# FFN way down in halves of 256 columns, block by block, with h at another address, and a new order of the last normalisation

## Chip, core and metric

One Trainium2 core runs the whole kernel. The metric is the device time of one execution in microseconds; the kernel before takes 991.96 us, the median of 3 runs (991.29 to 992.9).

## The reference, cut to what matters

One block of a model: a half-weighted FFN, a mixer, a second half-weighted FFN and a final RMS norm, all in float32, with 512 tokens, D = 1024 and D_FF = 2816.

```python
def swiglu(h, w_gate, w_up, w_down):
    return (jax.nn.silu(h @ w_gate) * (h @ w_up)) @ w_down

x = x + 0.5 * swiglu(rmsnorm(x, norm_ffn1[l]), w_ffn1_gate[l], w_ffn1_up[l], w_ffn1_down[l])
x = x + hybrid_mixer(rmsnorm(x, norm_mix[l]), ...)          # two kinds of attention, not touched here
x = x + 0.5 * swiglu(rmsnorm(x, norm_ffn2[l]), w_ffn2_gate[l], w_ffn2_up[l], w_ffn2_down[l])
return rmsnorm(x, norm_final)
```

## The kernel before, in words

Every float32 product is made of three matmuls (`mm3`, lines 100 to 103): each operand is split into a high part and the rest, and high times high, high times rest and rest times high are summed in PSUM. ScalarE makes the high part (`halves` line 92, `halves_of_x` line 236), VectorE the rest (lines 96 and 237). Such a group of three is called a triple here. Each matmul has its own weight load.

An FFN has 22 blocks of 128 hidden features. The first four (`plain`) go through 24 matmuls of 512 columns for the gate and 24 for the up product. The other 18 go in nine pairs (`pair`), by a Winograd-like scheme on halves: 14 steps per pair, each of 12 matmuls of 256 columns into half of a PSUM bank (names pu, pv, pw), with additions of weights by VectorE in between. A hidden block is kept as h, high and rest, in 16 buffers of 128x512 (`kept`, lines 265 to 270).

The way down (`down`, line 392) multiplies four kept blocks by the down weights, for each of the 8 output blocks d: four triples of 512 columns into one bank pd, and then `half_added` (line 531) by VectorE into x. The first way down comes in two groups of four output blocks; the last one of the first FFN (two hidden blocks) in groups of 4, 2 and 2. The four ways down between are made while pairs run: `mixed` (line 442) lays one block d after every four or so pair steps, 28 steps to 8 blocks (14 to 8 for the last). There `run(d)` issues nothing itself: it puts its triples on the list `waiting`, and `between` (line 437) takes them off one by one, after each pair step and, when more than four wait, in the middle of one too (lines 340 and 341). `held` keeps the first five steps free of them. `issue_after(self.in_pair.ins)` (line 419) holds a triple behind the pair's matmuls on TensorE.

`go` (line 465) walks the steps: loads run 12 steps ahead, sums 6, halves 4. All weights are fetched by SyncE's queue. The order of instructions on each engine is planned ahead by the framework with a simulated timeline (line 1234), within data dependences and the `issue_after` edges; on the chip each engine keeps that order.

Addresses: tiles of a pool lie one behind the other, pools too. Nearly all have a multiple of 256 bytes per partition; a `gap` tile of 64 bytes (line 218) stands between th3/tl3 and the other tiles of `sp`. So the pairs' weights (sph, spl) lie 64 bytes higher modulo 256 than their moving operands (th3, tl3, xo), and the way down's weights (whi, wlo) and its moving h are equal modulo 256.

The end (lines 1112 to 1159): x is turned by TensorE to token-major z, four row tiles i in two halves of 512 columns. For each i and half there are two triples of the last two hidden blocks (h is the stationary operand here), then `residual`: VectorE adds into z, ScalarE squares it with a running sum into ss. GpSimd makes the mean's first half and multiplies z by the gain in the first half. `norm(i)` follows at once: Sqrt by ScalarE, reciprocal by VectorE, one half scaled by ScalarE, the other by VectorE, and two DMAs out on SyncE's queue.

Of the kernel before, what the change touches and what calls it, by code (L numbers as in the profile page):

```python
# [9 lines left out]
F32 = mybir.dt.float32  # L10
# [5 lines left out]
S = 512  # L16
# [5 lines left out]
FP = 4  # L22
# [7 lines left out]
def block_kernel(ctx: ExitStack, tc: tile.TileContext, A: dict, out: bass.AP):  # L30
# [69 lines left out]
    def mm3(p, w, v, first, last, again=False):  # L100
        nc.tensor.matmul(p, w[0], v[0], start=first, stop=False, skip_group_check=again)  # L101
        nc.tensor.matmul(p, w[0], v[1], start=False, stop=False, skip_group_check=again)  # L102
        return nc.tensor.matmul(p, w[1], v[0], start=False, stop=last, skip_group_check=again)  # L103

    def mm2(p, w, v, first, last):

# [21 lines left out]

    gates = cp.tile([128, NT, 24], F32, name="gates")
    pos = cp.tile([128, 2, 32], F32, name="pos")  # L130
    ss = cp.tile([128, 2, NT], F32, name="ss")
# [3 lines left out]
    cp.tile([128, 48], F32, name="rest")  # L135
# [56 lines left out]
    class Ffn:  # L192
# [26 lines left out]

# [87 lines left out]
        def pair(self, f):  # L307
# [36 lines left out]
            def copied(m, to, name):  # L344
                part[m, name] = self.sp.tile([128, HT], F32, name="wc", tag="wc", bufs=4)
# [43 lines left out]
                                  lambda m=m, then=then: then(m)])  # L389
            return steps  # L390

        def down(self, w, fs, then, tags=("mm",), groups=(1,) * NK, kept_back=True, left=None):


            n = len(fs)
            raw, got, bank = {}, {}, {}

            def loads(d):
                if d % (8 // n) == 0:
                    raw[d * n // 8] = chunk((8, 128))  # L400
                    fetch(raw[d * n // 8], w[d * n // 8])

            def halves_of(d):
                if d % (4 // n) == 0:
                    i = d * n % 8
                    with self.behind_lo() if kept_back else nullcontext():
                        parts = halves(raw[d * n // 8][:, i:i + 4])
                    for k, v in enumerate(parts):
                        got[d + k // n, k % n] = v

            def run(d):
                ds = {sum(groups[:g]): range(sum(groups[:g]), sum(groups[:g + 1])) for g in range(len(groups))}.get(d)
                if ds is None:
                    return

                def triple(i, k):
                    if k == 0:
                        bank[i] = pt(tags[i % len(tags)], "pd")
                    with tc.issue_after(self.in_pair.ins) if left != 0 and self.in_pair else nullcontext():
                        mm3(bank[i], got[i, k], self.hs[fs[k]], k == 0, k == n - 1)  # L420
                    if k == n - 1:
                        then(i, bank[i])
# [4 lines left out]
                at = 0 if left is None else len(todo) - (left if ds[-1] == NK - 1 else 0)  # L427
                if at:
                    self.between(len(self.waiting))
                for one in todo[:at]:  # L430
                    one()
# [5 lines left out]
        def between(self, n):  # L437

            for _ in range(min(n, len(self.waiting))):
                self.waiting.pop(0)()  # L440

        def mixed(self, steps, fills, tail=1):

# [8 lines left out]
        def lay(self, wd):  # L452

            for f in range(FP):
                self.steps += self.plain(f)
            self.steps += self.down(wd[0], range(FP), half_added, ("s", "t", "o", "mm"), (4, 4), False, 1)
            fills = []
            for f in range(FP, NF, FP):
                fs = range(f, min(f + FP, NF))
                pairs = [step for i in fs[::2] for step in self.pair(i)]  # L460
                self.steps += self.mixed(pairs, fills) if fills else pairs
                if len(fs) == FP:
                    fills = self.down(wd[f // FP], fs, half_added)

        def go(self, after):
            steps, at = self.steps, [0, 0, 0]
            late, count = None, 0
            for i, s in enumerate(steps):
# [20 lines left out]
            self.between(len(self.waiting))  # L489


    scr_t = dp.tile([16, 128, RVW], F32, name="scr_t")
# [40 lines left out]
    with ExitStack() as ph:  # L533
# [55 lines left out]
            squares(tmp, d, "tmp", 5)  # L589

        ffn.lay(A["wd1a"])
        ffn.steps += ffn.down(A["wd1b"], range(NF - NF % FP, NF), then, (None,), (4, 2, 2), left=0)
        ffn.go(after)


# [495 lines left out]
    with ExitStack() as ph:  # L1091
# [41 lines left out]
        def norm(i):  # L1133
            r = ss[:, 1, i:i + 1]
            nc.scalar.activation(r, r, AF.Sqrt, bias=mean[:, i:i + 1], scale=1.0 / D)
            nc.vector.reciprocal(r, r)
            y = [xp.tile([128, S], F32, name="xo", tag="xo", bufs=16) for _ in range(2)]
            nc.scalar.activation(y[0], z[i, 0], AF.Copy, scale=r)
            nc.vector.scalar_tensor_tensor(y[1], z[i, 1], r, gf[1], ALU.mult, ALU.mult)
            for half in range(2):  # L1140
                nc.sync.dma_start(out[i * 128:(i + 1) * 128, half * S:(half + 1) * S], y[half])

        last = range(NF - NF % FP, NF)
        w = [load(A["wd2b"][half]) for half in range(2)]
# [2 lines left out]
                z[i, half] = turn_x(i, half)  # L1147
        for i in range(NT):
            b = slice(i * 128, (i + 1) * 128)
            for half in range(2):  # L1150
                p = pt(None, "pd")
                for k, f in enumerate(last):
                    mm3(p, (hs[f][0][:, b], hs[f][1][:, b]), w[half][k], f == last[0], f == last[-1])
                residual(i, half, p)
                if half == 0:
                    nc.gpsimd.tensor_scalar(mean[:, i:i + 1], ss[:, 0, i:i + 1], 1.0 / D, 1e-6, ALU.mult, ALU.add)
                    nc.gpsimd.tensor_tensor(z[i, 0], z[i, 0], gf[0], ALU.mult)
                else:
                    norm(i)


def _buckets(dist):
# [84 lines left out]
```

## Time and profile before

| | us |
|---|---|
| median of 3 runs | 991.96 |
| the profiled execution | 990.21 |
| its span, first to last instruction | 988.4 |
| mean granted TensorE clock | 0.997 of full speed |
| HBM read and written | 97.98 MB and 5.30 MB |
| the way down between pairs, stage by stage | about 124 to 331 and 750 to 960 |

All rows come from one profiled execution. Times in them are microseconds from the first instruction. TensorE's matmuls are pipelined: the duration in a row includes the drain, so the cost of one in a stream is the distance of its start to the next start. "PE" is the matmul, "PEld" the weight load that runs beside it, "DVE" VectorE, "ACT" ScalarE, "POOL" GpSimd, "SPq" the queue of SyncE. The name pd<-h,whi reads: written pd, read h and whi.

### The profile page before, as it was taken

To read this page: it belongs to the slowest core of one execution; us is meant where nothing else is said; L and a number is where in the kernel's file an instruction comes from. 1 tells how busy PE (TensorE), PEld (TensorE's weight loads), DVE (VectorE), ACT (ScalarE), POOL (GpSimd) and SP (SyncE) were. 2 spreads that over 40 slices of the span, in tenths; PEclk is the share of its full clock that TensorE was granted. 3 is DMA by queue.
4 is the path that set the end of the run, shared out by engine and by line. 5 is a ranking of instruction groups with operands and counts; after the bars stand their busy time and mean duration, and the time that the engine had idled before them with its cause. 6 is when DMAs were issued, how large, how long until landed. Compare 5 with 4: busy or idle time off the path is not lost.

```text
span 988.4 us, 16902 instructions
## 1 busy us (share of the span) xinstructions
PE 970.5 (98%) x6084; PEld 859.0 (87%) x6084; DVE 778.5 (79%) x1579; ACT 561.9 (57%) x1165; POOL 132.5 (13%) x176
## 2 busy tenths in 40 slices
PE   9999999999999999999999999999999999999996
PEld 7789999999999898787878888888999999999985
DVE  6996997688776587768788978789898788777744
ACT  6464655445544366567677886655475445454435
POOL 0000000000000000035666676100000000000002
PEclk9999999999999999999999999999999999999998
DMA  7255534332321125531121232226254322341102
GB/s 257 97 185 173 196 129 133 110 102 91 97 68 43 58 88 190 181 113 33 53 72 43 87 85 80 71 86 213 67 166 153 119 73 95 101 128 44 54 11 86
DMA packets 50056, 104.52 MB, mean 106 GB/s; under 512 B 10129, under 2 KB 14690, under 8 KB 49972
## 3 DMA queue, kind: packets, MB, share of 16 engines
q1 hardware_dynamic: 49684, 102.91, 32.4%
q8 instruction: 48, 0.79, 0.3%
q10 hardware_dynamic: 288, 0.52, 0.1%
q14 instruction: 36, 0.29, 0.1%
HBM read 97.98 MB, written 5.30 MB: 104 GB/s over the span
## 4 chain that ended last, share of the span: by engine, by line
PE 91%; DVE 4%; issue 1%; ACT 1%; DMA 1%; POOL 0%; SPq 0%; POOLq 0%; ACTq 0%; DVEq 0%
PE pd L102 8%; PE pd L103 8%; PE pd L101 8%; PE pu L101 6%; PE pu L103 6%; PE pu L102 6%; PE pw L101 4%; PE pw L103 4%; PE pw L102 4%; PE pp L103 3%; PE pp L101 3%; PE pp L102 3%; PE pgu L102 3%; PE pgu L101 3%; PE pgu L103 3%; PE ps_t L940 3%
## 5 line engine op out<-in xcount | busy, mean ns | idle before, releaser
L236 ACT ACTIVATE sph<-aw 128x512 fp32r<-128x512 f32 x252 | 157.3, 630 | 197.4 <-PE pu L102 71.1
L237 DVE TENSOR_TENSOR spl<-aw,sph 128x512 fp32r<-128x512 f32 x252 | 172.3, 690 | 59.7 <-ACT sph L236 57.2
L92 ACT ACTIVATE whi<-raw 128x512 fp32r<-128x512 f32 (+1 forms) x200 | 121.5, 619 | 126.4 <-PE pd L102 44.2
L102 PE MATMUL pd<-h,whi 128*128 128x512 f32 x336 | 132.7, 395 | 0.0
L103 PE MATMUL pd<-h,wlo 128*128 128x512 f32 x336 | 131.1, 393 | 0.0
L96 DVE TENSOR_TENSOR wlo<-raw,whi 128x512 fp32r<-128x512 f32 (+1 forms) x168 | 111.7, 676 | 24.1 <-ACT whi L92 20.6
L101 PE MATMUL pd<-h,whi 128*128 128x512 f32 x336 | 130.4, 394 | 0.0
L101 PE MATMUL pu<-th,sph 128*128 128x256 f32 x432 | 119.4, 276 | 0.3 <-ACT wc L346 0.3
L103 PE MATMUL pu<-th,spl 128*128 128x256 f32 x432 | 119.4, 276 | 0.0
L102 PE MATMUL pu<-tl,sph 128*128 128x256 f32 x432 | 119.2, 276 | 0.0
L322 DVE TENSOR_TENSOR aw<-aw 128x512 f32<-128x512 f32 x144 | 99.0, 689 | 0.0
L531 DVE SCALAR_TENSOR_TENSOR x<-pd,x 128x512 f32<-128x512 f32 x88 | 60.1, 689 | 33.3 <-PE pd L103 33.3
L101 PEld LDWEIGHTS pu<-th,sph 128*128 128x128 f32 x432 | 81.1, 188 | 4.6 <-ACT wc L346 0.5
L102 PEld LDWEIGHTS pu<-tl,sph 128*128 128x128 f32 x432 | 81.1, 188 | 4.0
L103 PEld LDWEIGHTS pu<-th,spl 128*128 128x128 f32 x432 | 81.1, 188 | 0.1
L101 PE MATMUL pw<-xo,sph 128*128 128x256 f32 x288 | 79.7, 277 | 0.2 <-ACT sph L236 0.2
L102 PE MATMUL pw<-xo,sph 128*128 128x256 f32 x288 | 79.5, 276 | 0.0
L103 PE MATMUL pw<-xo,spl 128*128 128x256 f32 x288 | 79.4, 277 | 0.0
L103 PEld LDWEIGHTS pd<-h,wlo 128*128 128x128 f32 x336 | 63.1, 188 | 13.8
L102 PEld LDWEIGHTS pd<-h,whi 128*128 128x128 f32 x336 | 63.1, 188 | 4.0
L101 PEld LDWEIGHTS pd<-h,whi 128*128 128x128 f32 x336 | 63.1, 188 | 3.7
L101 PEld LDWEIGHTS pw<-xo,sph 128*128 128x128 f32 x288 | 54.1, 188 | 3.9 <-ACT sph L236 0.6
(246 smaller groups left out, 2443.1 us busy)
## 6 DMA issues: line engine op xcount, KB each, us to landing
aw<-in_wg SPq DMA_DIRECT2D x72, 256.0 KB, 2.8
aw<-in_wu SPq DMA_DIRECT2D x72, 256.0 KB, 4.5
raw<-in_wd1a SPq DMA_DIRECT2D x20, 512.0 KB, 3.9
raw<-in_wd2a SPq DMA_DIRECT2D x20, 512.0 KB, 4.8
raw<-in_w_a SPq DMA_DIRECT2D x16, 512.0 KB, 4.8
raw<-in_w SPq DMA_DIRECT2D x8, 512.0 KB, 4.0
raw<-in_w_o SPq DMA_DIRECT2D x8, 512.0 KB, 3.6
raw<-in_wg SPq DMA_DIRECT2D x7, 512.0 KB, 3.6
```

The costliest lines, as they stand in the source:

```text
L92: last_hi[0] = nc.scalar.activation(hi, v, AF.Copy)
L96: nc.vector.tensor_tensor(lo, v, f32(hi), ALU.subtract)
L101: nc.tensor.matmul(p, w[0], v[0], start=first, stop=False, skip_group_check=again)
L102: nc.tensor.matmul(p, w[0], v[1], start=False, stop=False, skip_group_check=again)
L103: return nc.tensor.matmul(p, w[1], v[0], start=False, stop=last, skip_group_check=again)
L236: nc.scalar.activation(hi, v, AF.Copy)
L237: self.last_lo = nc.vector.tensor_tensor(lo, v, f32(hi), ALU.subtract)
L322: nc.vector.tensor_tensor(to, x, y, op)
L531: nc.vector.scalar_tensor_tensor(xs[d], p, 0.5, xs[d], ALU.mult, ALU.add)
L940: nc.tensor.transpose(p[:, wide:wide + 128], lps[qi][:, j * 128:(j + 1) * 128], ident)
```

## The change

In `down`, a block of its own (the four ways down between the pairs) is now made at once, in two halves of 256 columns: for each half the four triples of that half, 24 matmuls where there were 12. `waiting`, `between`, `held` and `in_pair` are gone, so no triple stands inside or between pair steps other than in whole blocks. In `go` nothing is left over at the end. The first way down and the last one keep 512 columns and their groups; their banks are now taken from all four tags in turn.

A tile of 192 bytes (`gap_h`) ahead of h and one of 64 bytes (`gap_t`) ahead of th3/tl3 move h by 192 bytes modulo 256 and leave all else where it was modulo 256; `ss` grows and `rest` shrinks by as much. The way down's weights thereby lie 64 bytes higher modulo 256 than h, as the pairs' do.

At the end the second half of the last row tile is split in two parts of 256 columns, each with its own bank, residual and square; their sums meet in a small VectorE operation. `norm(i - 1)` is issued after the matmuls of tile i. Two edges hold a norm's reciprocal behind the newest residual, and its VectorE scaling behind that small sum. The very last first-half output goes out on ScalarE's queue.

```diff
@@ class Ffn, __init__
-            self.waiting = []
-            self.in_pair = None
-            self.held = 5
+            hp.tile([128, 48], F32, name="gap_h", tag="gap_h", bufs=1)
+            sp.tile([128, 16], F32, name="gap_t", tag="gap_t", bufs=1)
@@ pair, run
-                    self.in_pair = mm3(bank[m, to], (hi[:, k], lo[:, k]), x, first and k == 0, k == 3, not first)
-                    if k == 1:
-                        self.between(self.held == 0 and len(self.waiting) > 4)
-                self.between(self.held == 0)
-                self.held = max(self.held - 1, 0)
+                    mm3(bank[m, to], (hi[:, k], lo[:, k]), x, first and k == 0, k == 3, not first)
@@ down, run
-                todo = []
-                for ks in ([range(n)] if len(ds) == 1 else [range(n - 1), range(n - 1, n)]):
-                    todo += [lambda i=i, k=k: triple(i, k) for i in ds for k in ks]
...
-                self.waiting += todo[at:]
+                for i in ds:
+                    bank[i] = pt(tag, "pd")
+                if len(ds) == 1:
+                    for cols in (slice(0, HT), slice(HT, S)):
+                        for k in range(n):
+                            mm3(bank[d][:, cols], got[d, k], [v[:, cols] for v in self.hs[fs[k]]], k == 0, k == n - 1)
+                else:
+                    for ks in (range(n - 1), range(n - 1, n)):
+                        for i in ds:
+                            for k in ks:
+                                mm3(bank[i], got[i, k], self.hs[fs[k]], k == 0, k == n - 1)
+                for i in ds:
+                    then(i, bank[i])
@@ the end
-        def residual(i, half, p):
-            nc.vector.scalar_tensor_tensor(z[i, half], p, 0.5, z[i, half], ALU.mult, ALU.add)
-            nc.scalar.activation(sq, z[i, half], AF.Square, accum_out=ss[:, half, i:i + 1])
+        def residual(i, part, p, cols):
+            v = z[i, min(part, 1)][:, cols]
+            added[0] = nc.vector.scalar_tensor_tensor(v, p, 0.5, v, ALU.mult, ALU.add)
+            nc.scalar.activation(sq[:, cols], v, AF.Square, accum_out=ss[:, part, i:i + 1])
...
+            with tc.issue_after(added[0].ins):
+                nc.vector.reciprocal(r, r)
...
+            with tc.issue_after(summed_up[0].ins) if summed_up[0] else nullcontext():
+                nc.vector.scalar_tensor_tensor(y[1], z[i, 1], r, gf[1], ALU.mult, ALU.mult)
             for half in range(2):
-                nc.sync.dma_start(out[i * 128:(i + 1) * 128, half * S:(half + 1) * S], y[half])
+                queue = nc.scalar if i == NT - 1 and half == 0 else nc.sync
+                queue.dma_start(out[i * 128:(i + 1) * 128, half * S:(half + 1) * S], y[half])
...
+            parts = [slice(0, S), slice(0, S)] if i < NT - 1 else [slice(0, S), slice(0, S // 2), slice(S // 2, S)]
+            for part, cols in enumerate(parts):
+                p = pt(None, "pd")[:, cols]
...
+                residual(i, part, p, cols)
...
+                elif part < len(parts) - 1:
+                    summed_up[0] = nc.vector.scalar_tensor_tensor(
+                        mean[:, i:i + 1], ss[:, 1, i:i + 1], 1.0 / D, mean[:, i:i + 1], ALU.mult, ALU.add)
+            if i:
+                norm(i - 1, 1)
+        norm(NT - 1, 2)
```

## Rows read from the trace of the kernel before

**Rows 1.** The page, busy time of each engine over the span.
```profile
PE 970.5 (98%) x6084; PEld 859.0 (87%) x6084; DVE 778.5 (79%) x1579; ACT 561.9 (57%) x1165; POOL 132.5 (13%) x176
```
**Rows 2.** Busy time by stage: length, PE, PEld, DVE, ACT, POOL (count), clock, DMA share, GB/s.
```profile
124.00:331.00 207.00, 207.00 (x1461) 191.41 (x1460) 158.55 (x277) 100.63 (x194) 0.00 (x0) 1.00 0.30 94
712.00:750.00 38.00, 37.78 (x328) 37.45 (x327) 33.85 (x62) 25.69 (x52) 0.00 (x0) 1.00 0.45 149
750.00:960.00 210.00, 210.00 (x1475) 193.87 (x1474) 159.83 (x279) 100.03 (x194) 0.00 (x0) 1.00 0.27 89
```
**Rows 3.** Groups by line, TensorE, 124 to 331: shapes xcount | busy, mean ns | idle.
```profile
L102 PE MATMUL pd<-h,whi 128*128 128x512 f32 x116 | 46.1, 397 | 0.0
```
**Rows 4.** The same group from 750 to 960.
```profile
L102 PE MATMUL pd<-h,whi 128*128 128x512 f32 x120 | 47.7, 397 | 0.0
```
**Rows 5.** TensorE in order of time (start, duration), triples between steps of 256 columns.
```profile
302.80 0.40 PE L101 MATMUL pd<-h,whi 128*128 128x512 f32 x1
...
303.50 0.28 PE L101 MATMUL pv<-xo,sph 128*128 128x256 f32 x1
...
304.18 0.40 PE L101 MATMUL pd<-h,whi 128*128 128x512 f32 x1
```
**Rows 6.** TensorE in order of time, inside a long run of 512 columns.
```profile
690.74 0.39 PE L101 MATMUL pd<-h,whi 128*128 128x512 f32 x1
...
692.10 1.07 PE L101 MATMUL pd<-h,whi 128*128 128x512 f32 x4
```
**Rows 7.** TensorE in order of time, pairs alone, second FFN, and their first triple.
```profile
709.97 0.28 PE L103 MATMUL pw<-xo,spl 128*128 128x256 f32 x1
...
711.97 0.40 PE L101 MATMUL pd<-h,whi 128*128 128x512 f32 x1
...
713.46 0.28 PE L103 MATMUL pu<-th,spl 128*128 128x256 f32 x1
```
**Rows 8.** TensorE in order of time, a wait in the second FFN's pairs.
```profile
743.88 0.39 PE L101 MATMUL pu<-xo,sph 128*128 128x256 f32 x1 [0.22 <-ACT t L368]
744.10 0.28 PE L102 MATMUL pu<-xo,sph 128*128 128x256 f32 x1
...
745.28 0.28 PE L103 MATMUL pu<-xo,spl 128*128 128x256 f32 x1
```
**Rows 9.** TensorE in order of time, behind two waits in the first FFN's pairs.
```profile
109.70 0.28 PE L102 MATMUL pu<-tl,sph 128*128 128x256 f32 x1
...
110.84 0.28 PE L103 MATMUL pu<-th,spl 128*128 128x256 f32 x1
```
**Rows 10.** The end in order of time: TensorE's last matmul.
```profile
979.84 0.39 PE L103 MATMUL pd<-whi,h 128*128 128x512 f32 x1
```
**Rows 11.** The end in order of time: VectorE.
```profile
981.18 0.16 DVE L1136 RECIPROCAL ss<-ss 128x1 f32<-128x1 f32 x1 [0.64 <-ACT ss L1135]
981.26 0.67 DVE L1130 SCALAR_TENSOR_TENSOR z<-pd,z 128x512 f32<-128x512 f32 x1
...
983.60 0.75 DVE L1139 SCALAR_TENSOR_TENSOR xo<-z,ss,gf 128x512 f32<-128x512 f32 x1
```
**Rows 12.** The end in order of time: ScalarE.
```profile
981.67 0.71 ACT L1138 ACTIVATE xo<-z,ss 128x512 f32<-128x512 f32 x1
...
983.08 0.29 ACT L1135 ACTIVATE ss<-ss,mean 128x1 f32<-128x1 f32 x1
983.75 0.72 ACT L1138 ACTIVATE xo<-z,ss 128x512 f32<-128x512 f32 x1 [0.37 <-POOL z L1157]
```
**Rows 13.** The end in order of time: GpSimd.
```profile
982.12 1.60 POOL L1157 TENSOR_TENSOR z<-z,gf 128x512 f32<-128x512 f32 x1
```
**Rows 14.** The end in order of time: SyncE's issues of the eight outputs, merged.
```profile
977.20 8.10 SPq L1141 DMA_DIRECT2D out<-xo  x8
```
**Rows 15.** Groups by line and shape, VectorE, 712 to 750: 256 columns.
```profile
L350 DVE TENSOR_TENSOR t<-pv,wc 128x256 f32<-128x256 f32 x3 | 1.2, 422 | 0.0
```
**Rows 16.** Groups by line and shape, ScalarE, 735 to 989: 256 columns.
```profile
L346 ACT ACTIVATE wc<-pu 128x256 f32<-128x256 f32 x28 | 10.3, 369 | 2.4 <-PE pu L103 2.4
```

More of the change, by code (lines that the diff above doesn't have):

```diff
@@ L102, in mm3 @@
         nc.tensor.matmul(p, w[0], v[1], start=False, stop=False, skip_group_check=again)
-        return nc.tensor.matmul(p, w[1], v[0], start=False, stop=last, skip_group_check=again)
+        nc.tensor.matmul(p, w[1], v[0], start=False, stop=last, skip_group_check=again)
     def mm2(p, w, v, first, last):
@@ L130, in block_kernel @@
     pos = cp.tile([128, 2, 32], F32, name="pos")
-    ss = cp.tile([128, 2, NT], F32, name="ss")
+    ss = cp.tile([128, 3, NT], F32, name="ss")
     mean = cp.tile([128, NT], F32, name="mean")
@@ L134, in block_kernel @@
     far = cp.tile([32, 16], F32, name="far")
-    cp.tile([128, 48], F32, name="rest")
+    cp.tile([128, 40], F32, name="rest")
     ones_f = cp.tile([128, 128], F32, name="ones_f")
@@ L390, in pair, with down @@
             return steps
-        def down(self, w, fs, then, tags=("mm",), groups=(1,) * NK, kept_back=True, left=None):
+        def down(self, w, fs, then, tag="mm", groups=(1,) * NK, kept_back=True):
             n = len(fs)
@@ L414, in run @@
                     return
[L416 to L422, printed above, removed]
-                todo = []
-                for ks in ([range(n)] if len(ds) == 1 else [range(n - 1), range(n - 1, n)]):
-                    todo += [lambda i=i, k=k: triple(i, k) for i in ds for k in ks]
[L427 to L431, printed above, removed]
-                self.waiting += todo[at:]
+                for i in ds:
[11 more added lines that the diff above has]
+                    then(i, bank[i])
             return [[lambda d=d: loads(d), None, lambda d=d: halves_of(d), lambda d=d: run(d), None, True]
                     for d in range(NK)]
-        def between(self, n):
-            for _ in range(min(n, len(self.waiting))):
-                self.waiting.pop(0)()
         def mixed(self, steps, fills, tail=1):
@@ L455, in lay @@
                 self.steps += self.plain(f)
-            self.steps += self.down(wd[0], range(FP), half_added, ("s", "t", "o", "mm"), (4, 4), False, 1)
+            self.steps += self.down(wd[0], range(FP), half_added, None, (4, 4), False)
             fills = []
@@ L488, in go @@
                 late()
-            self.between(len(self.waiting))
     scr_t = dp.tile([16, 128, RVW], F32, name="scr_t")
@@ L591, in block_kernel @@
         ffn.lay(A["wd1a"])
-        ffn.steps += ffn.down(A["wd1b"], range(NF - NF % FP, NF), then, (None,), (4, 2, 2), left=0)
+        ffn.steps += ffn.down(A["wd1b"], range(NF - NF % FP, NF), then, None, (4, 2, 2))
         ffn.go(after)
@@ L1126, in block_kernel, with norm @@
         z = {}
[L1128 to L1134 removed]
+        summed_up = [None]
+        def residual(i, part, p, cols):
+            v = z[i, min(part, 1)][:, cols]
+            added[0] = nc.vector.scalar_tensor_tensor(v, p, 0.5, v, ALU.mult, ALU.add)
+            nc.scalar.activation(sq[:, cols], v, AF.Square, accum_out=ss[:, part, i:i + 1])
+        def norm(i, part):
+            r = ss[:, part, i:i + 1]
             nc.scalar.activation(r, r, AF.Sqrt, bias=mean[:, i:i + 1], scale=1.0 / D)
[L1136 removed]
+            with tc.issue_after(added[0].ins):
+                nc.vector.reciprocal(r, r)
             y = [xp.tile([128, S], F32, name="xo", tag="xo", bufs=16) for _ in range(2)]
             nc.scalar.activation(y[0], z[i, 0], AF.Copy, scale=r)
[L1139 removed]
+            with tc.issue_after(summed_up[0].ins) if summed_up[0] else nullcontext():
+                nc.vector.scalar_tensor_tensor(y[1], z[i, 1], r, gf[1], ALU.mult, ALU.mult)
             for half in range(2):
[L1141 removed]
+                queue = nc.scalar if i == NT - 1 and half == 0 else nc.sync
+                queue.dma_start(out[i * 128:(i + 1) * 128, half * S:(half + 1) * S], y[half])
         last = range(NF - NF % FP, NF)
@@ L1149, in block_kernel @@
             b = slice(i * 128, (i + 1) * 128)
-            for half in range(2):
-                p = pt(None, "pd")
+            parts = [slice(0, S), slice(0, S)] if i < NT - 1 else [slice(0, S), slice(0, S // 2), slice(S // 2, S)]
+            for part, cols in enumerate(parts):
+                p = pt(None, "pd")[:, cols]
                 for k, f in enumerate(last):
-                    mm3(p, (hs[f][0][:, b], hs[f][1][:, b]), w[half][k], f == last[0], f == last[-1])
-                residual(i, half, p)
-                if half == 0:
+                    mm3(p, (hs[f][0][:, b], hs[f][1][:, b]), [v[:, cols] for v in w[min(part, 1)][k]],
+                        f == last[0], f == last[-1])
+                residual(i, part, p, cols)
+                if part == 0:
                     nc.gpsimd.tensor_scalar(mean[:, i:i + 1], ss[:, 0, i:i + 1], 1.0 / D, 1e-6, ALU.mult, ALU.add)
                     nc.gpsimd.tensor_tensor(z[i, 0], z[i, 0], gf[0], ALU.mult)
-                else:
-                    norm(i)
+                elif part < len(parts) - 1:
[4 more added lines that the diff above has]
+        norm(NT - 1, 2)
 def _buckets(dist):
```

## Prediction

> **What bounds the kernel now.** I read the busy table first: TensorE is busy for 98% of the span, VectorE for 79% [rows 1]. The stage table says where that is tightest: in the two stages in which ways down and pairs are mixed TensorE is busy for all of 207.00 and all of 210.00 us, while VectorE has 158.55 and 159.83 [rows 2]. There no wait counts; only the number of matmuls and the distance from one start to the next do. So I took these distances from the timeline. At the very end it is the other way round: TensorE's last matmul ends at 979.84 + 0.39 = 980.23, and 8.2 us of the span follow; there the chain through VectorE, ScalarE, GpSimd and the outputs' DMAs sets the end [rows 10 to 14].
>
> **The distances.** In a long run of 512 columns, six matmuls take 692.10 - 690.74 = 1.36 us, 0.227 each [rows 6]. Six matmuls of 256 columns between two triples take 304.18 - 303.50 = 0.68, 0.113 each [rows 5]. Two of 256 thus cost what one of 512 costs in a run. But a single triple of 512 among matmuls of 256 takes 303.50 - 302.80 = 0.70 us, and six of 256 would take 0.68 [rows 5]: each triple loses 0.02 us by its neighbours. Nearly every triple of the ways down between the pairs stands like that: 116 in one stage and 120 in the other [rows 3, 4].
>
> There is a second pace of 256 columns. Ahead of the triple at 711.97, 17 matmuls take 711.97 - 709.97 = 2.00 us, 0.1176 each; the triple and the seven behind it take 1.49, which is 0.70 and seven times 0.113 [rows 7]. So the triple brought the fast pace back. Behind a wait of 0.22 us ScalarE caused, ten take 745.28 - 744.10 = 1.18, the slow pace again [rows 8]; behind two other waits ten take 110.84 - 109.70 = 1.14, the fast one [rows 9]. The slow pace costs 4.3 ns per matmul of 256 columns, without any wait in the record.
>
> **The change, part by part.**
>
> *Halves, block by block.* Removed: 768 matmuls of 512 columns (2 FFNs, 4 ways down, 8 blocks, 4 triples, 3 each). Added: 1536 of 256. At the fast pace this is the same time, and the loss at the seams goes: 236 x 0.02 = 4.7 us. What could take from it is a fixed price per matmul; 2 x 0.113 against 0.227 leaves none [rows 5, 6]. The Trainium skill, "TensorE: Matmul & The Clock Gate", section "Back-to-back issue gap", does give one: columns / 2.4 plus about 2.5 ns, so that 768 more matmuls would cost 1.9 us, an estimate from that page; by it this part would bring 2.8 us in place of 4.7, and the rows of this case, with no such difference, decide for 4.7.
>
> VectorE and ScalarE get no operation more here; `half_added` comes once per block as before. What changes is the slack: four pair steps now follow each other without triples between, and then a block takes 24 x 0.113 = 2.7 us. The nearest stage is the pairs alone: there VectorE is busy for 33.85 of 38.00 us, 89%, and TensorE still for 37.78 [rows 2]. Waits there sum to 0.22 us in 28 steps. In the mixed stages VectorE has more room (77%), and halves run four steps ahead. I allow 0.5 us for new waits in all; bounds 0 and 5.4 (the rival below).
>
> *h at another address.* No operation is added. What it does to a matmul no row shows alone: runs of 512 with equal addresses modulo 256 and runs of 256 with 64 bytes between both have full pace [rows 5, 6]. For the halves I take the pairs' 0.113, because after the move their addresses stand as the pairs' do. For the 240 matmuls that keep 512 columns with h moving (two first ways down of 96, one last of 48) I take no change; if all had the isolated triple's 0.70 / 3 = 0.233 instead of 0.227, 1.6 us are lost. Bounds 0 and 1.6.
>
> *The pace of 256 columns.* I leave as much at the slow pace as before. Bounds: [rows 7, 8] show 27 matmuls at it, 0.1 us; were the time from there to the next triple all slow, some 0.7 us in all could be gained; or the rival below.
>
> *The end.* Before, VectorE's reciprocal of tile 2 waited for ScalarE's Sqrt and stood ahead of the last residual, which so began at 981.26, 1.03 us after TensorE's end [rows 10, 11]. Then ScalarE was still scaling tile 2 until 981.67 + 0.71 = 982.38 [rows 12]; Sqrt, reciprocal and the second half's scaling ended at 983.60 + 0.75 = 984.35 [rows 11], the first half at 983.75 + 0.72 = 984.47, released by GpSimd, whose product of 982.12 to 983.72 came late because the squares did [rows 12, 13]. SyncE then issued the two last outputs one behind the other until 977.20 + 8.10 = 985.30 [rows 14].
> After: the last residual has 256 columns, 0.42 us [rows 15], and may begin at 980.27; the square of that width some 0.37 [rows 16] plus about 0.15 for its sum and hand-over; Sqrt 0.29, reciprocal 0.16, scaling 0.75 [rows 11, 12], with 0.05 to 0.1 between: 980.27 + 0.42 + 0.10 + 0.52 + 0.08 + 0.29 + 0.03 + 0.16 + 0.03 + 0.75 = 982.65, 1.7 us ahead of before. Scaling of tile 2 may stand in that chain (0.71 on ScalarE or 0.75 on VectorE): then 1.0 ahead. The last output's issue no longer waits behind another on SyncE, some 0.4 more. GpSimd's product depends on the first half's residual and square, which lose the reciprocal ahead of them as well; it should end by about 982.3, and the first half 0.72 later, 1.4 ahead. Queued behind the held reciprocal is VectorE's scaling of the earlier tile; nobody but an output waits for it. The small sum waits for a square and may hold the last residual by about 0.3. I take 1.6 us gained; bounds 2.3 gained and 0.3 lost (the chain with both scalings ahead and the table load of ScalarE moved into it).
>
> *Where the path ends at the last pair.* The chain from the last pair's matmul to its h is covered by the last block (2.7 us) and the transposes of the first half of x, in place of triples held back; I cost it at nothing, 0.5 us if the cover fails.
>
> **Sum.** 990.21 - 4.7 - 1.6 + 0.5 = 984.4 for an execution like the profiled one. That one stands 1.75 us under the median, so 986.2 for the median.
>
> **The rivals.**
>
> *The slow pace stays (slower).* The change takes away every lone triple, and one of these ended the slow pace [rows 7]. If a wait as at 743.88 [rows 8] leaves the slow pace behind and nothing ends it, the second FFN's mixed stage runs at it: 7 pairs x 168 + 768 = 1944 matmuls x 4.3 ns = 8.4 us, 994.6. All 4560 matmuls of 256 columns of both FFNs: 19.6 us, 1005.8. It outweighs the gain from 5.8 / 0.0043 = 1350 matmuls on. For it: that pace lasted [rows 8]. Against it: the pace behind the other two waits was the fast one [rows 9], the mixed stages have no wait now, and with equal addresses for pairs and halves a run may keep what it has. The Trainium skill has a rule that speaks for this rival ("TensorE: Matmul & The Clock Gate", section "LDWEIGHTS (loading the stationary operand)"): a load of 128 columns takes 128 / 1.2, 107 ns, and that leaves 6 ns beside 113, while 512 columns leave 120; the trace's busy weight loads, 191.41 of 207.00 us, agree that little is left [rows 2]. Chance 0.25.
>
> *Waits take the triples' place.* Without a triple between two steps on the same bank, each of the 14 mixed pairs waits once as at 743.88, where the start is some 0.39 us late: 5.4 us, 991.1. For it: the one such wait was in pairs alone [rows 8]. Against: 28 steps there had only that one. Chance 0.10.
>
> *The seam's loss only moves.* If a 256-column half loses at the block's edge or by its addresses what the triple lost, only the end gains: 986.2 + 4.7 = 990.9. Chance 0.10.
>
> **How the numbers follow.** The forecast, 986.2, has 0.55; its own range is 984 to 989. A difference under 0.2% (2 us) can't be told from none here: faster is under 990.0, slower over 993.9. Faster: 0.55, and 0.03 of the third rival where the end brings more: 0.58. Slower: 0.20 of the slow pace and 0.03 of the waits: 0.23. Same: the rest, 0.19. The range is 983.5 (all bounds on the good side but one) to 995.5: it takes in both middle rivals and the slow pace in one mixed stage, and leaves out slow pace in both.
>
> **What would show it.** In the after profile, right: no pd of 512 columns between 124 and 960 other than in groups; 12 starts of pd and pairs in 1.36 us all through the mixed stages; the two stages together some 4.7 us shorter; the last residual starting within 0.1 us of TensorE's end. Wrong: starts 0.1176 apart for long stretches (first rival), waits of TensorE on wc, t or sph in the mixed stages (second), pd starts more than 0.113 apart with pairs at 0.113 (third).

## The result and the profile after

The changed kernel takes 997.8 us, the median of four runs (996.8 to 1000.4); the kernel before takes 991.6 beside it. The ratio is 1.0064, interval 1.0050 to 1.0077: slower by 6.2 us, where 986.2 was forecast and 983.5 to 995.5 was the range.

The busy table of after looks like before's [rows 1]; TensorE has 774 matmuls more and is busy for 7.8 us longer.

```profile
span 996.0 us, 18460 instructions
...
PE 978.3 (98%) x6858; PEld 900.7 (90%) x6858; DVE 784.6 (79%) x1581; ACT 565.3 (57%) x1167; POOL 133.1 (13%) x176
```

The two mixed stages by stage (length, PE, PEld, VectorE, ScalarE, GpSimd, with counts; granted clock; DMA share; GB/s):

```profile
124.00:331.00 207.00, 207.00 (x1780) 207.00 (x1779) 160.30 (x276) 100.57 (x192) 0.00 (x0) 1.00 0.31 95
750.00:960.00 210.00, 210.00 (x1807) 210.00 (x1806) 163.21 (x282) 102.49 (x197) 0.00 (x0) 1.00 0.27 87
```

TensorE is busy for every microsecond of both, as before [rows 2], and the granted clock is 1.00, the 2.4 GHz level. No start of a pair or a way down there is more than 40 ns late, before or after: the change put no wait there. And the busy share cannot say where 7.6 us of span came from. Summing the span between landmarks of the two traces can: from the first FFN's first pair to its last triple of the way down 280.3 us became 284.8 (+4.5), the same stretch of the second FFN up to TensorE's end 283.8 became 287.0 (+3.2), the two first ways down together +0.8, the end after TensorE's last matmul 8.20 became 7.72 (-0.5), all else -0.4. The loss lies inside the stages that were to gain.

The timeline of TensorE in the second FFN (start, duration) shows how. Pairs alone first, then the first matmuls of a way down, then pairs again:

```profile
737.33 0.28 PE L103 MATMUL pu<-th,spl 128*128 128x256 f32 x1
...
738.69 0.28 PE L103 MATMUL pu<-th,spl 128*128 128x256 f32 x1
...
738.91 0.28 PE L102 MATMUL pw<-xo,sph 128*128 128x256 f32 x1
739.03 0.28 PE L101 MATMUL pd<-h,whi 128*128 128x256 f32 x1
739.15 0.28 PE L102 MATMUL pd<-h,whi 128*128 128x256 f32 x1
...
739.74 0.28 PE L101 MATMUL pu<-th,sph 128*128 128x256 f32 x1
...
740.92 0.28 PE L102 MATMUL pu<-tl,sph 128*128 128x256 f32 x1
```

Twelve matmuls take 738.69 - 737.33 = 1.36 us, 0.113 each, ahead of the first pd. From that pd on, ten take 740.92 - 739.74 = 1.18, 0.118 each: the slow pace of [rows 7, 8], entered at a seam (the border between matmuls of a pair and of a way down), with no wait. It stays for 9.5 us. Two late starts in the pairs, distances of 0.15 and 0.22 us, bring the fast pace back (19 matmuls in 752.04 - 749.89 = 2.15 us), and the next matmul of a block, at 752.04, ends it again:

```profile
749.04 0.28 PE L101 MATMUL pv<-xo,sph 128*128 128x256 f32 x1
749.20 0.38 PE L101 MATMUL pu<-xo,sph 128*128 128x256 f32 x1
749.42 0.28 PE L102 MATMUL pu<-xo,sph 128*128 128x256 f32 x1
...
749.89 0.28 PE L103 MATMUL pu<-xo,spl 128*128 128x256 f32 x1
...
752.04 0.28 PE L103 MATMUL pd<-h,wlo 128*128 128x256 f32 x1
```

Much later, between two blocks:

```profile
783.76 0.28 PE L101 MATMUL pw<-xo,sph 128*128 128x256 f32 x1
...
786.58 0.28 PE L101 MATMUL pd<-h,whi 128*128 128x256 f32 x1
...
787.05 0.28 PE L102 MATMUL pd<-h,whi 128*128 128x256 f32 x1
...
787.39 0.28 PE L102 MATMUL pd<-h,whi 128*128 128x256 f32 x1
```

24 matmuls of a pair take 786.58 - 783.76 = 2.82 us (0.1175 each); the block's first four still take 0.47 (786.58 to 787.05, 0.1175 each), the next three 0.34, the fast pace. So here a block regains the fast pace inside itself, and the pairs behind it lose it again. This is the rule in after: of the 90 stretches of pair matmuls behind a block, 88 begin slow, though 69 of the blocks ahead of them had ended fast. (A block needn't stand whole: the planned order lets pair matmuls in between.)

For every kernel I then took each start-to-start distance over the nominal one, 0.1133 us for 256 columns and 0.2267 for 512 [rows 5, 6], and summed what was over. A matmul counts as slow if it is late by more than 2.5 ns. Waits (over 40 ns) are left out of this table; in the pairs they sum to 1.8 us before and 1.7 after. The columns: pairs (3024 matmuls), the way down's matmuls of 256 and of 512 columns, and the span that follows TensorE's last matmul.

| kernel | pairs slow | over, us | pd of 256: slow of, over | pd of 512: over, us | end, us | median, us |
|---|---|---|---|---|---|---|
| before | 175 | 0.8 | none | 4.9 | 8.20 | 991.6 to 992.8 |
| after | 2370 | 10.7 | 339 of 1536, 2.1 | 1.6 | 7.72 | 997.8 |
| halves_h0 | 2999 | 13.6 | 1536 of 1536, 10.0 | 0.2 | 7.67 | 1007.3 |
| triples_h192 | 478 | 3.0 | none | 4.0 | 8.15 | 992.9 |
| end_alone | 262 | 1.3 | none | 4.9 | 8.78 | 992.1 |
| halves_pairs_addr | 3002 | 13.3 | 1536 of 1536, 6.8 | 0.2 | 7.96 | 1004.1 |
| lone_once | 74 | 0.3 | 1 of 1536, 0.0 | 0.2 | 7.95 | 983.7 |
| groups_pairs_addr (its profile) | 2 | 0.0 | 1 of 1536, 0.0 | 1.3 | 7.95 | 996.0 |
| whole_h0 | 2666 | 11.9 | none | 2.1 | 7.50 | 997.4 |
| whole_h192 | 407 | 2.2 | none | 6.0 | 7.60 | 993.3 |
| lone_other_addr | 2506 | 11.4 | 1536 of 1536, 10.0 | 0.2 | 7.66 | 1007.0 |

Before to after: the triples' 4.9 us became 2.1 + 1.6, and the pairs' 0.8 became 10.7. That is +8.6, and with the end's -0.5 it is 8.1, where the span grew by 7.6: the pace accounts for all of the loss, to within 0.5 us.

### The profile page after: what moved, and what is told of

Read it like the earlier page. It is cut to its first block, busy times and chain, and to the rows that moved or that the text cites. A ratio compares the mean times of both kernels' runs of the same rounds, so it can differ in the third digit from the quotient of the medians.

```text
span 996.0 us, 18460 instructions
## 1 busy us (share of the span) xinstructions
PE 978.3 (98%) x6858; PEld 900.7 (90%) x6858; DVE 784.6 (79%) x1581; ACT 565.3 (57%) x1167; POOL 133.1 (13%) x176
## 4 chain that ended last, share of the span: by engine, by line
PE 94%; DVE 3%; issue 1%; ACT 1%; DMA 0%; DVEq 0%; ACTq 0%
PE pd L103 8%; PE pd L101 8%; PE pd L102 8%; PE pu L101 7%; PE pu L103 7%; PE pu L102 7%; PE pw L101 5%; PE pw L103 5%; PE pw L102 5%; PE pp L103 3%; PE pgu L101 3%; PE pgu L102 3%; PE pp L101 3%; PE pp L102 3%; PE pgu L103 3%; PE pv L101 3%
## 5 line engine op out<-in xcount | busy, mean ns | idle before, releaser
L102 PE MATMUL pd<-h,whi 128*128 128x256 f32 (+1 forms) x592 | 173.4, 293 | 0.0
L103 PE MATMUL pd<-h,wlo 128*128 128x256 f32 (+1 forms) x592 | 173.1, 293 | 0.0
L101 PE MATMUL pd<-h,whi 128*128 128x256 f32 (+1 forms) x592 | 171.7, 293 | 0.0
L96 DVE TENSOR_TENSOR wlo<-raw,whi 128x512 fp32r<-128x512 f32 (+1 forms) x168 | 111.1, 671 | 23.5 <-ACT whi L92 19.8
L102 PEld LDWEIGHTS pd<-h,whi 128*128 128x128 f32 x592 | 111.3, 188 | 3.5
L103 PEld LDWEIGHTS pd<-h,wlo 128*128 128x128 f32 x592 | 111.3, 188 | 3.5
L101 PEld LDWEIGHTS pd<-h,whi 128*128 128x128 f32 x592 | 111.1, 188 | 3.3
L101 PE MATMUL pw<-xo,sph 128*128 128x256 f32 x288 | 80.7, 280 | 0.0
L102 PE MATMUL pw<-xo,sph 128*128 128x256 f32 x288 | 80.6, 280 | 0.0
```

The lines of the kernel that those rows point to most:

```text
L96: nc.vector.tensor_tensor(lo, v, f32(hi), ALU.subtract)
```

## The experiments

Three theories, and where each puts the cause. A: the width; a triple of 512 columns is needed now and then, and any kernel without lone triples is slow. B: the moved h; the halves would be good without it. C: the pace is handed on from matmul to matmul; it changes only where width or place in memory changes, a lone triple of 512 brings the fast one, and a stream that keeps width and places keeps what it has. "Places" are addresses modulo 256 in a partition. In the built programs the pairs' weights stand at 96 and their moving operands at 32. The way down has weights 32 and h 32 before, weights 32 and h 224 after: the same difference of 64 as the pairs, at other places.

**halves_h0**: the change without the move of h.

```diff
-            hp.tile([128, 48], F32, name="gap_h", tag="gap_h", bufs=1)
-            sp.tile([128, 16], F32, name="gap_t", tag="gap_t", bufs=1)
```

> The changed kernel with h left at its old address (gap_h and gap_t taken out); halves, block by block, and the new end stay. Theory A (widths: without a lone triple of 512 columns nothing ends the slow pace of 256 columns): pairs run mostly at 0.1176 us per matmul as in the changed kernel, time 996 to 1000 us. Theory B (addresses: moving h put the slow pace there): pairs back at 0.113, time 986 to 989 us.

Measured: 1007.3 us, ratio 1.0143 (1.0128 to 1.0158). Nearly all pairs run at the slow pace, and the blocks are slower still: 10.0 us over 1536 matmuls, 6.5 ns each, 0.120. A block's last 15 take 840.53 - 838.73 = 1.80 us:

```profile
838.73 0.28 PE L101 MATMUL pd<-h,whi 128*128 128x256 f32 x1
...
840.53 0.28 PE L101 MATMUL pu<-th,sph 128*128 128x256 f32 x1
```

The time is above both forecasts: no theory had a price for blocks slower than the slow pace. B falls: the halves are worse without the moved h, by 9.5 us. The move cured most of what the halves brought.

**triples_h192**: the reverse, the kernel before with the two gap tiles and nothing else.

> The kernel before with nothing but h moved by 192 bytes modulo 256; lone triples of 512 columns between the pair steps stay. Theory A (widths): pairs stay at 0.113 us, the groups of 512 go from 0.227 to 0.233, time 992 to 994 us. Theory B (addresses): pairs go to 0.1176 behind the triples, some 10 us more, about 1001 us.

Measured: 992.9 us, ratio 1.0005 (0.9996 to 1.0014): the move alone costs nothing that can be told from none. A triple between pairs, in its timeline:

```profile
801.25 0.39 PE L101 MATMUL pd<-h,whi 128*128 128x512 f32 x1
...
801.94 0.28 PE L101 MATMUL pv<-xo,sph 128*128 128x256 f32 x1
```

It takes 0.69 us where [rows 5] had 0.70; the long runs of 512 go from 0.228 to 0.233, as A said; and 478 pair matmuls are slow in place of 175, mostly two behind each triple and then fast again. Over nominal the 512 columns win 0.9 us (4.9 to 4.0) and the pairs lose 2.2.

**end_alone**: the kernel before with only the new end (three `ss` columns, the split last half, the edges and the queue, as in the change).

> The kernel before with nothing but the new end (last half in two parts, norm one tile later, VectorE's edges, one output on ScalarE's queue). By the changed kernel's trace, where TensorE's end to the span's end went from 8.20 to 7.72 us: 0.5 us faster, 991 us. By the recorded prediction: 1.6 us faster, 990 us.

Measured: 992.1 us, ratio 0.9997 (0.9988 to 1.0007). The recorded 1.6 us lies outside this interval (1.2 us faster to 0.7 slower), 0.5 us inside it. So the end brings 1.2 us at most; in its trace 8.78 us follow TensorE's last matmul, more than the 8.20 before.

**halves_pairs_addr**: halves_h0, with the blocks' weights in the pairs' own buffers, so that pairs and blocks agree in width and in both places (96 and 32).

```diff
-    def halves(src):
+    def halves(src, pool=None, names=("whi", "wlo"), bufs=5):
...
+                        own = (self.sp, ("sph", "spl"), 6) if len(groups) == NK else ()
+                        parts = halves(raw[d * n // 8][:, i:i + 4], *own)
```

> As halves_h0, and the ways down between pairs keep their split weights in the pairs' own buffers (sph, spl), so that moving operand and weights lie at the same places modulo 256 (32 and 96) in pairs and in blocks. Theory A (widths): pairs mostly at 0.1176, 996 us or more. Theory B (addresses): no seam at all, pairs and blocks at 0.113, 4.7 us of the seams and 0.5 of the end gained, about 986 us; waits may come in since 6 buffers now serve both.

Measured: 1004.1 us, ratio 1.0107 (1.0092 to 1.0122). A block and the pair behind it, in the second FFN:

```profile
759.02 0.28 PE L103 MATMUL pd<-h,spl 128*128 128x256 f32 x1
...
760.43 0.28 PE L103 MATMUL pd<-h,spl 128*128 128x256 f32 x1
760.55 0.28 PE L103 MATMUL pw<-xo,spl 128*128 128x256 f32 x1
...
761.73 0.28 PE L101 MATMUL pw<-xo,sph 128*128 128x256 f32 x1
```

Twelve of the block in 1.41 and ten of the pair in 1.18: one pace, 0.118, on both sides of the seam, and so from the first pair to the last. At equal places the seam does nothing. But this stream came out of its run of 512 columns at the slow pace, and nothing in it ends that. B's 986 us falls once more. This is what C needs, and A too; the next one tells them apart.

**lone_once**: halves_pairs_addr, and in each FFN one single triple of 512 columns, the last of the first way down, is held back until five steps of the first pair are made. One triple per FFN, none after it.

```diff
+            self.waiting, self.in_pair, self.held = [], None, 5
...
+                self.held -= 1
+                if self.held == 0:
+                    self.waiting.pop(0)()
...
+                    def last_one(i=ds[-1], k=n - 1):
+                        with tc.issue_after(self.in_pair.ins):
+                            mm3(bank[i], got[i, k], self.hs[fs[k]], False, True)
+                        then(i, bank[i])
```

> As halves_pairs_addr, but the last triple of the first way down (512 columns, at the old addresses) is held back until five pair steps have run, once per FFN. Theory C (the pace is handed on from matmul to matmul; a lone triple brings the fast one, equal places modulo 256 and equal width keep what there is): fast from there to the end of each FFN, 1004.1 - 19.5 = 984.6 us; 993 if a wait throws one FFN back. Theory A (256 columns are slow unless triples of 512 keep coming): 1003 us.

Measured: 983.7 us (982.9 to 984.5), ratio 0.9909 (0.9892 to 0.9925). It beats both kernels; against halves_pairs_addr it gains 20.4 us by moving two triples. Between the two profiled executions the gain is 19.8 us of span, and the table's 13.0 at the pairs and 6.8 at the halves are all of it. The lone triple of the second FFN:

```profile
704.95 0.28 PE L103 MATMUL pu<-xo,spl 128*128 128x256 f32 x1
...
707.66 0.39 PE L101 MATMUL pd<-h,whi 128*128 128x512 f32 x1
...
708.36 0.28 PE L101 MATMUL pu<-th,sph 128*128 128x256 f32 x1
...
709.72 0.28 PE L103 MATMUL pw<-xo,spl 128*128 128x256 f32 x1
```

Ahead of it 23 take 707.66 - 704.95 = 2.71 us, 0.118 each; behind it 12 take 709.72 - 708.36 = 1.36, 0.113. Blocks and pairs some 73 us later:

```profile
780.43 0.28 PE L101 MATMUL pu<-th,sph 128*128 128x256 f32 x1
...
783.15 0.28 PE L101 MATMUL pd<-h,sph 128*128 128x256 f32 x1
...
784.86 0.28 PE L101 MATMUL pd<-h,sph 128*128 128x256 f32 x1
784.97 0.28 PE L101 MATMUL pu<-th,sph 128*128 128x256 f32 x1
...
786.10 0.28 PE L102 MATMUL pu<-tl,sph 128*128 128x256 f32 x1
```

24 of a pair in 2.72, 16 of a way down in 1.82, ten of the pair behind in 1.13: 0.113 throughout; over both FFNs one of 81 pair stretches behind a block begins slow. And the stage's busy row says the same "all of it" as the slow kernels' do, here of its 712 to 950:

```profile
712.00:950.00 238.00, 238.00 (x2103) 238.00 (x2102) 192.79 (x337) 126.23 (x241) 0.00 (x0) 1.00 0.31 99
```

With 74 slow matmuls of 3024, A in its plain form (triples are needed now and then) falls; one is enough, if the places agree.

**lone_other_addr**: lone_once with the weights back in `whi` and `wlo` (place 32). Meant to change the place alone, it changes three things beside: the difference to h is 0 in place of 64, the weights have buffers of their own again, and the planned order brings the first block some 90 pair matmuls sooner.

```diff
-                        own = (self.sp, ("sph", "spl"), 6) if len(groups) == NK else ()
-                        parts = halves(raw[d * n // 8][:, i:i + 4], *own)
+                        parts = halves(raw[d * n // 8][:, i:i + 4])
```

> As lone_once, but the ways down between pairs keep their weights in whi and wlo again (32 modulo 256, h at 32, pairs at 96 and 32). Theory C (fast pace is kept only where places modulo 256 are the pairs' own): the first mixed block throws the pairs back to 0.1176 and blocks run at 0.120 as in halves_h0, 1003 to 1007 us. Rival (one lone triple is all that the changed kernel lacked): 984 to 988 us.

Measured: 1007.0 us, ratio 1.0151 (1.0137 to 1.0165), 23.3 us over lone_once. Between the profiled executions it is 23.4: 11.1 at the pairs, 10.0 at the halves, 2.6 of waits in the pairs, of which lone_once has none, and -0.3 at the end. Its pairs are fast up to the first block, 12 starts in 1.36:

```profile
735.75 0.28 PE L101 MATMUL pu<-xo,sph 128*128 128x256 f32 x1
...
737.11 0.28 PE L101 MATMUL pw<-xo,sph 128*128 128x256 f32 x1
```

In the first FFN they are slow from the first block on. In the second they come back to the fast pace some ten matmuls behind the first matmuls of a block (744.14), and lose it for good at a wait ahead of the next ones (757.68):

```profile
754.75 0.39 PE L101 MATMUL pu<-xo,sph 128*128 128x256 f32 x1 [0.63 <-ACT t L365]
```

Behind every later block the pairs are slow. In all 2506 of 3024 are, and every pd. So C as worded is too narrow: a late start can change the pace too, to the fast one (749.20 in after) or to the slow one (here), as [rows 8, 9] had shown. Groups by line and shape (count; busy us, mean ns of one; idle) of lone_once, then of lone_other_addr:

```profile
L101 PE MATMUL pd<-h,sph 128*128 128x256 f32 x512 | 141.3, 276 | 0.0
...
L101 PE MATMUL pu<-th,sph 128*128 128x256 f32 x432 | 119.2, 276 | 0.0
```

```profile
L101 PE MATMUL pd<-h,whi 128*128 128x256 f32 x512 | 144.8, 283 | 0.0
...
L103 PE MATMUL pu<-th,spl 128*128 128x256 f32 x432 | 121.1, 280 | 0.0
```

The mean duration shows the pace too, 276 against 280 and 283 ns, once one knows to look at 4 ns. The changed kernel has 278 for pd and 280 for pu:

```profile
L101 PE MATMUL pd<-h,whi 128*128 128x256 f32 x512 | 142.1, 278 | 0.0
...
L103 PE MATMUL pu<-th,spl 128*128 128x256 f32 x432 | 121.1, 280 | 0.0
```

**whole_h0 and whole_h192**: the change with blocks of 512 columns, block by block, without and with the moved h (the edit is against halves_h0 and against the change).

```diff
-                    for cols in (slice(0, HT), slice(HT, S)):
+                    for cols in (slice(0, S),):
```

> The changed kernel with blocks of 512 columns instead of halves and h at its old address: of the change only the order by blocks, the end and the banks are left. Theory C: long runs of 512 hand on the slow pace, so pairs behind blocks are slow, blocks at 0.227: before - 4.7 - 0.5 + 1.3 for new seams + 10 to 13 for the pairs, 998 to 1001 us. If halves are the cause: 988 us.

> The changed kernel with blocks of 512 columns instead of halves, h moved. Theory C: blocks at 0.233 (5 us more than at 0.227), the pairs behind them fast as in the first pairs of the changed kernel: 992 to 993 us. If order by blocks makes pairs slow whatever the addresses: 1002 us or more.

Measured: whole_h0 997.4 us, ratio 1.0049 (1.0034 to 1.0064), 2666 pairs slow; whole_h192 993.3, ratio 1.0011 (1.0002 to 1.0021), 407 slow, but its pd of 512 columns are 6.0 us over. So 512 columns in a block don't bring the fast pace by themselves, at h's old place; at the new one they do and then run at about 0.233 each themselves. A falls here too: whole_h0 has 512 columns between its pairs and is slow, whole_h192 has no lone triple and is mostly fast. C had both paces right; its 998 to 1001 for whole_h0 was 0.6 us too high. Of the four kernels made block by block with weights in whi and wlo (256 or 512 columns, h moved or not) only 512 with h moved leaves the pairs mostly fast. Width is not the cause alone, and neither is the place.

**groups_pairs_addr**: halves_pairs_addr, with the first way down's weights in the pairs' buffers as well, so that even the run of 512 columns ahead of the pairs has their places; no lone triple.

```diff
-                        own = (self.sp, ("sph", "spl"), 6) if len(groups) == NK else ()
+                        own = (self.sp, ("sph", "spl"), 6) if kept_back is False or len(groups) == NK else ()
```

> As halves_pairs_addr, but the first way down, in its groups of 512 columns, keeps its weights in the pairs' buffers too, 64 bytes ahead of h. Theory C, with the pace at entry set by the long run of 512: it runs at 0.233 as in the changed kernel (1.2 us more) and hands the fast pace on, 986 us. If the run of 512 columns hands on the slow pace whatever its addresses: 1005 us.

Measured: median 996.0 us, ratio 1.0001 (0.9966 to 1.0035, without the highest run), but the ten runs lie at three levels: 985.8 to 987.7 (four), 995.8 to 997.9 (five), 1006.2 (one). The steps are 10 us, and lone_once against halves_pairs_addr, with both FFNs switched, is 20.4. So it looks as if each FFN came out of its 512-column run fast or slow by chance and then kept that pace for its whole length. The one that was profiled is of the lowest level, with 2 slow pairs of 3024; of the others there is no trace, so this is inferred from times. That profile shows that the fast pace can come without a lone triple; with one, all 14 runs of lone_once and of the two kernels below took 982.6 to 984.9. Undecided: what tips it.

**lone_old_end** (lone_once with the end of before) and **lone_end_vector**, which is lone_once with

```diff
-                    nc.gpsimd.tensor_tensor(z[i, 0], z[i, 0], gf[0], ALU.mult)
+                    (nc.vector if i == NT - 1 else nc.gpsimd).tensor_tensor(z[i, 0], z[i, 0], gf[0], ALU.mult)
```

> As lone_once with the end of the kernel before. By end_alone (0.9997 of before) the new end is worth 0 to 0.8 us: 983.7 to 984.5 us. If the new end only pays once TensorE's path ends elsewhere: 1.5 us or more slower than lone_once.

> As lone_once, but the last row tile's product of z with the gain runs on VectorE and not on GpSimd. In the changed kernel VectorE's small sum took 1.00 us, until GpSimd's product ended, and the last norm waited for it. If that wait is what kept the end from its 1.6 us: 0.5 to 0.9 us faster than lone_once, 983.0. If another step is as late: within 0.2 us of it.

Measured: 984.7 (983.0 to 984.9), ratio 0.9922 (0.9909 to 0.9934), and 983.8, ratio 0.9917 (0.9903 to 0.9931), beside lone_once's 983.7. The three can't be told apart: neither the 1.5 us or more of the one forecast nor the 0.5 to 0.9 of the other shows, and end_alone's bound on the new end stays the best. In the trace of lone_end_vector 7.32 us follow TensorE's end in place of lone_once's 7.95, but TensorE itself ends 0.73 us later in that execution: a gain of 0.6 is below what these times resolve.

## Why the prediction was wrong, and where it was right

**The pace at the seams: the failed step.** The prediction read both paces from the rows and made "the slow pace stays" its first rival, at 994.6 for one mixed stage and 1005.8 for both FFNs. What came is this rival: 10.7 us at the pairs and 2.1 at the halves, 12.8 of its 19.6 (0.8 of which was there before). Two sentences sent the forecast the other way. "For the halves I take the pairs' 0.113, because after the move their addresses stand as the pairs' do": their difference does, their places don't. After has the pairs' difference and loses the pace at its seams; lone_once has their places too and keeps it. With the weights back at 32 (lone_other_addr) 21.1 us are lost to the pace, though there the difference and the order changed as well. "I leave as much at the slow pace as before": the rival was given a wait as its only door ("if a wait as at 743.88 leaves the slow pace behind"), and "the mixed stages have no wait now" then spoke against it. The mixed stages have no wait in after either; the door was the seam itself, 738.91 to 739.15, which the change makes between unlike places around each of 32 blocks per FFN. The door that was named exists (754.75 in lone_other_addr), but in after's mixed stages it was not used. That single triples ended the slow pace [rows 7] was seen, and that all of them would be gone was written down; it should have weighed more than the absence of waits.

The range's upper end, 995.5, was drawn to leave out the slow pace in both FFNs, though it had been priced at 1005.8, and 997.8 fell between the two. Its lower end does not follow from the bounds given either: 986.2 - 0.5 - 0.7 - 0.7 is 984.3, not 983.5.

By terms, for the profiled executions, 984.4 was forecast and 997.8 came, 13.4 us more: 11.9 of pace, 1.4 of h, 1.1 of the end, less 0.6 of waits that did not come, 13.8 in all. The median misses by less, 11.6, because 1.75 us were added for it, and the profiled execution of after lies at its median: luck.

**The seams' 4.7 us: right in size, then paid out again.** Before, the ways down's 512-column matmuls lose 4.9 us over nominal; in lone_once the halves lose nothing (one late start of 1536). So twice as many matmuls of half the width cost nothing here. The Trainium skill ("TensorE: Matmul & The Clock Gate", "Back-to-back issue gap") gives columns / 2.4 plus some 2.5 ns for one matmul, by which 768 more would cost 1.9 us, an estimate from that page. The rows of lone_once show none of that: both widths keep the same 0.44 ns per column.

**h at another address: inside the bounds, at the bad one.** For the 240 matmuls that stay at 512 columns I took no change and bounds 0 and 1.6. Measured 1.6 over nominal, where halves_h0, with h at its old address, has 0.2. In after's first way down of the second FFN:

```profile
698.04 0.39 PE L102 MATMUL pd<-h,whi 128*128 128x512 f32 x1
...
698.98 0.39 PE L102 MATMUL pd<-h,whi 128*128 128x512 f32 x1
```

Four starts in 0.94 us by these rounded times; the whole run of 48 from 690.11 to 701.30 has 0.233 each, against 0.227 [rows 6].

**The end: 1.6 us forecast, 0.5 in after's trace, nothing measurable in end_alone.** The order came as predicted: the last residual starts at 988.30, 0.03 us after TensorE's end at 987.99 + 0.28. The end of after in order of time:

```profile
988.30 0.42 DVE L1115 SCALAR_TENSOR_TENSOR z<-pd,z 128x256 f32<-128x256 f32 x1 [0.25 <-PE pd L103]
...
988.85 1.27 POOL L1147 TENSOR_TENSOR z<-z,gf 128x512 f32<-128x512 f32 x1
...
989.13 1.00 DVE L1149 SCALAR_TENSOR_TENSOR mean<-ss,mean 128x1 f32<-128x1 f32 x1 [0.34 <-ACT sqd L1116]
...
990.06 0.74 DVE L1126 SCALAR_TENSOR_TENSOR xo<-z,ss,gf 128x512 f32<-128x512 f32 x1
...
990.90 0.75 DVE L1126 SCALAR_TENSOR_TENSOR xo<-z,ss,gf 128x512 f32<-128x512 f32 x1
990.97 0.72 ACT L1124 ACTIVATE xo<-z,ss 128x512 f32<-128x512 f32 x1 [0.44 <-DVE ss L1122]
991.72 0.38 ACTq L1129 DMA_DIRECT2D out<-xo  x1
```

Three terms were missed. The small sum of one column takes 1.00 us, and ends at 990.13 as GpSimd's product does (988.85 + 1.27 = 990.12); the chain had it inside 0.15 for sum and hand-over. Without that product on GpSimd it takes 0.15, in lone_end_vector:

```profile
976.38 0.15 DVE L1163 SCALAR_TENSOR_TENSOR mean<-ss,mean 128x1 f32<-128x1 f32 x1
```

Second, VectorE's scaling of tile 2, of which the prediction said that nobody but an output waits for it, starts at 990.06 behind that sum; the last Sqrt ends at 990.23 + 0.29 = 990.52, but the last reciprocal starts at 990.72 and the last scaling at 990.90, behind it. The case with one scaling in the chain had been named, at 1.0 us gained in place of 1.7; the 1.6 was taken all the same.

And the last output's landing: the last issue came 1.2 us earlier against TensorE's end than before, but the last output landed 3.18 us after it (994.93), where before it was 2.57. Now the last two leave within 0.03 us of each other from two queues, which is my reading of the 0.6; no run took that apart. Other traces fit it: 2.25 us in lone_old_end with one queue, 2.82 in lone_end_vector and 3.20 in end_alone with two.

**No waits in place of triples: right.** Allowed 0.5 us, and in the mixed stages no start of pairs or ways down is more than 40 ns late. The second rival fell. The third, "the seam's loss only moves", is what the halves did in part (2.1 of 4.9), but at its 990.9 it missed the pairs.

**What stays open.** What makes the two paces: the busy time of the weight loads, which the prediction read for its first rival, is full in after (207.00 of 207.00) and in lone_once (238.00 of 238.00) alike and doesn't tell them apart. Whether the place of the moving operand matters or only that of the weights: lone_other_addr and lone_once moved the weights, and after against halves_h0 moved h, which also changed the pace (2.1 against 10.0 us over in the halves), so neither seems without effect. Each of these moves changed the difference too: that the difference is not enough follows from after and lone_once, what it is worth by itself no run shows. Why one late start ends the slow pace and another the fast one. Why a run of 512 columns at the pairs' places lets each FFN out fast or slow.

## What to carry to other kernels

Where a TensorE stage is busy for 100%, read the start-to-start distance of its matmuls, not the share: two paces 4% apart both show as full. When work of another kind is put between streams, follow the distance across the seam and ask what ended the slow stretches before; if the edit removes that, price the slow pace to the end of the stage and keep it in the range. Here the best form was: same width, both operands at the same places modulo 256 in pairs and blocks, and one lone 512-column triple to set the pace, 983.7 us against 992.4 for the kernel before beside it.

## What the runs showed of the hardware that was not expected

- TensorE has two steady paces for float32 products of 256 columns at the same granted clock of 1.00, 0.113 and 0.118 us, and a third of 0.120 at some places; with equal places it kept either one over a whole FFN's pairs and blocks (halves_pairs_addr and lone_once run the same matmuls but for the position of two triples, 20.4 us apart).
- A way down with the pairs' difference of weight and moving addresses modulo 256, but at other places, throws the pairs to the slow pace (88 of 90 stretches behind a block in after); with the pairs' own places it doesn't (1 of 81 in lone_once).
- A one-column VectorE operation took 1.00 us beside a GpSimd product and 0.15 without it. The Trainium skill ("SBUF — State Buffer", "Who interferes with whom") has it that a VectorE instruction with two SBUF inputs contends with a GpSimd instruction that reads SBUF. After's trace agrees: the two end within 0.01 us of each other.
